# Weight splits and weight sums of a hybrid decoder layer, put in program order on their engines

## The chip, the cores and the metric

The kernel runs on one core of a Trainium2 chip. The metric is the device time of one execution in microseconds (us). Of several executions the median is given.

## The reference

One layer of a hybrid decoder, sequence 256, width D = 2048, FFN width 5632, all in float32. The change bears on the two SwiGLU FFNs; between them stands the mixer (differential attention beside a Mamba-2 scan).

```python
def swiglu(x, w_gate, w_up, w_down):
    return (jax.nn.silu(x @ w_gate) * (x @ w_up)) @ w_down
...
        f = swiglu(rms_norm(h, ffn1_pre_g[i]), ffn1_w_gate[i], ffn1_w_up[i], ffn1_w_down[i])
        h = h + 0.5 * rms_norm(f, ffn1_post_g[i])
        u = rms_norm(h, mix_pre_g[i])
...
        h = h + rms_norm(merged @ w_out[i], mix_post_g[i])
        f = swiglu(rms_norm(h, ffn2_pre_g[i]), ffn2_w_gate[i], ffn2_w_up[i], ffn2_w_down[i])
        h = h + 0.5 * rms_norm(f, ffn2_post_g[i])
```

## The kernel before, in words

**Products.** Every float32 weight block is loaded from HBM and split into two parts: hi, its value rounded to the multiply's input type (`split`, L130, an activation on ACT), and lo, the rest (L131, a subtraction on DVE that reads the block and hi). The activations are split likewise. A product is then three matmuls (hi by hi, hi by lo, lo by hi), in `gate_up` the lines L384, L385 and L386. L385 is the only one that reads a weight's lo. PE runs its instructions in the order in which they stand.

**FFN.** `gate_up` makes one block j of 256 columns of gate and up, j = 0 to 10 (NFF = 11). The blocks stand in groups (0 to 2, 3 to 5, 6 to 8, 9 and 10), and after each group a `project` multiplies by the down weights. For one j, eight pairs p of row blocks are gone through in an order: `ORDER_D` for the first j of a group, `ORDER` for the seven others (1, 2, 4, 5, 7, 8, 10).

```python
ORDER = (2, 0, 4, 1, 6, 3, 5, 7)
ORDER_D = (0, 2, 1, 4, 3, 6, 5, 7)
```

The pairs 2, 4 and 6 (SP) are *summed units*, S here, from j = 1 on: their 2x2 block product is made from seven products in place of eight, with sums of the weights and of the activations. The pairs 0, 1, 3, 5 and 7 are plain, N here. So a j with ORDER runs S N S N S N N N. An N unit has two weight splits of 128x1024, a and b, and 24 matmuls. An S unit has 21 matmuls and four splits: a (of raw columns 0 and 1), b (of the sums e0 and e1), d (of the sum e2, 128x512) and c (of raw columns 2 and 3, the last already replaced by a sum). Its products come in the order a, a, b, b, d, c, c; in the first S unit of a j the second product of a (`u0`) comes after d.

**Sums.** The class `Ahead` loads the raw block of an S unit into one of two buffers (`raw7`, L362) and has POOL make the sums with four adds of 128x512 (L366): e0 = raw0 + raw3, e1 = e0 + raw1, e2 = raw1 + raw3, raw3 = e1 + raw2. The e's lie in `wsum`, one of two buffers with the tags xc0 and xc1. `make` for the S unit after next is called where c of the present one has been split, which frees its raw buffer.

**Order.** A scheduler sets each engine's order from priorities: splits and sums stand under `high_priority(offset=AHEAD)` (AHEAD = 300), which lets them move forward; data dependencies and buffers hold. `issue_after(i)` adds an order edge: what is inside comes after i. The split results lie in a ring of four buffers for 128x1024 (tags w) and of two for 128x512 (tags one).

**Start.** While j = 0 runs, which has no S units, the squares of x are summed in `square1` (L520 to L525): four tiles, added on DVE into the first, which lies in xc0, and halved there twice. `scale1` then has PE sum it over the partitions (`ss`, L530, in PSUM), DVE scales (L110), POOL takes the power -1/2 (L111), and the result `pre_rstd` scales gate and up in L441 (ACT, silu) and L442 (DVE), which read the PSUM banks of a finished j.

Of the kernel before, what the change touches and what calls it, by code (L numbers as in the profile page):

```python
# [22 lines left out]
F32 = mybir.dt.float32  # L23
F32R = mybir.dt.float32r
AF = mybir.ActivationFunctionType
ALU = mybir.AluOpType
AX = mybir.AxisListType

P = 128
# [16 lines left out]
TT = NT * P  # L46
# [6 lines left out]
def decoder_layer(ctx: ExitStack, tc: tile.TileContext, x, x_t, cols, rows, post_g, wgu1, wd1, w_in,  # L53
                  w_in_t, w_dt, w_att, w_ssm, w_out, wgu2, wd2, out):
    nc = tc.nc
# [7 lines left out]
    tmp = E(name="tmp", bufs=12)  # L63
# [6 lines left out]
    def turn(tag, n):  # L70

        turns[tag] = (turns.get(tag, -1) + 1) % n
        return f"{tag}{turns[tag]}"
# [12 lines left out]
    ones = const.tile([P, P], F32, name="ones")  # L86
# [26 lines left out]
    loaded = [None]  # L113
    ahead = [AHEAD]
    queue = []

    def split(raw, shape, parts=1, before=None):
        tag = turn("one", 2) if shape[1:] == [S] else turn("w", 4)
        hi, lo = (wsplit.tile(shape, F32R, name=f"w_{p}", tag=f"{p}_{tag}") for p in ("hi", "lo"))
        k = shape[1] // parts  # L120
        with ExitStack() as st:
            if ahead[0] and not queue:
                st.enter_context(tc.high_priority(offset=ahead[0]))
            for i in queue.pop(0) if queue else ():
                st.enter_context(tc.issue_after(i.ins))
            for a in range(0, shape[1], k):
                js = slice(a, a + k)
                if before:
                    before(js)
                nc.scalar.activation(hi[:, js], raw[:, js], AF.Copy)  # L130
                nc.vector.tensor_tensor(out=lo[:, js], in0=raw[:, js], in1=hi[:, js].bitcast(F32), op=ALU.subtract)  # L131
        return hi, lo

    def matmul3(ps, sl, j, t, wh, wl, first, last):
# [5 lines left out]
    def project(xs, w, n, by_token=0):  # L140

        ps = [psm.tile([P, S], F32, name="acc", tag="m") for _ in range(NT)]
        tail = []
        for c in range(len(xs)):
            raw = raws.tile([P, 4, S], F32, name="raw", tag=turn("raw", 3))
            loaded[0] = nc.sync.dma_start(raw, w(n, c))
            sl = xs[c] = xs[c]() if callable(xs[c]) else xs[c]
            for b in range(2):  # L150
                hi, lo = split(raw[:, 2 * b:2 * b + 2], [P, 2, S])
                for jj in range(2):
                    j = 2 * b + jj
                    tail.append((sl, j, hi[:, jj], lo[:, jj], c + j == 0, c == len(xs) - 1 and j == 3))
            if c < len(xs) - by_token:
                for sl_, j, wh, wl, first, last in tail:
                    for t in range(NT):
                        matmul3(ps[t], sl_, j, t, wh, wl, first, last)
                tail = []
        for t in range(NT):  # L160
            for sl_, j, wh, wl, first, last in tail:
                matmul3(ps[t], sl_, j, t, wh, wl, first, last)
        return ps

    def project_t(xs, w, n):

        ps = [psm.tile([P, 2 * TT], F32, name="acc", tag="m") for _ in range(2)]
        for b in range(len(xs)):
            if b % 2 == 0:
                raw = raws.tile([P, 8, 256], F32, name="raw", tag=turn("raw", 3))  # L170
                nc.sync.dma_start(raw, w(n, b // 2))
            hi, lo = split(raw[:, 4 * (b % 2):4 * (b % 2) + 4], [P, 4, 256])
            sl = xs[b].rearrange("p j i t -> p j (i t)")
            for j in range(4):
                wf = [slice(f * P, (f + 1) * P) for f in range(2)]
                for f in range(2):
                    nc.tensor.matmul(ps[f], hi[:, j, wf[f]], sl[:, j], start=b + j == 0, stop=False)  # L177
                for f in range(2):
                    nc.tensor.matmul(ps[f][:, TT:], lo[:, j, wf[f]], sl[:, j, :TT], start=False,  # L179
                                     stop=b == len(xs) - 1 and j == 3)  # L180
        out = tmp.tile([P, 2, TT], F32, name="pt", tag="t2")
        for f in range(2):
            nc.scalar.activation(out[:, f], ps[f][:, TT:], AF.Copy)
            nc.vector.tensor_tensor(out=out[:, f], in0=ps[f][:, :TT], in1=out[:, f], op=ALU.add)
        return out
# [55 lines left out]
    def inv_rms(s1):  # L241

        rstd = const.tile([P, NT], F32, name="pre_rstd", tag="rstd")
        rsqrt(rstd, s1, D)
        return rstd
# [54 lines left out]
    class pair_slots:  # L300
# [8 lines left out]
        def make(self, p, src, gain):  # L309

            g = col[:, gain + 2 * p:gain + 2 * p + 2]
            kind = p in SP[:-1]
            if kind not in self.free:
                self.free[kind] = new_slot()
                sl, k = self.free[kind], 0
            else:
                sl, k = self.free.pop(kind), 2
            self.at0[p] = sl, k
            if p in SP:
                xg = self.xg[p] = tmp.tile([P, 2, TT], F32, name="xg", tag="t2")  # L320
                for i in range(2):
                    nc.scalar.activation(xg[:, i], src[:, i], AF.Copy, scale=g[:, i:i + 1])
                fill(sl, k, xg)
            else:
                self.at[p] = sl, k
                for i in range(2):
                    nc.scalar.activation(sl[:, k + i, 0], src[:, i], AF.Copy, scale=g[:, i:i + 1])
                    nc.vector.scalar_tensor_tensor(
                        out=sl[:, k + i, 1], in0=src[:, i], scalar=g[:, i:i + 1],
                        in1=sl[:, k + i, 0].bitcast(F32), op0=ALU.mult, op1=ALU.subtract)  # L330
# [15 lines left out]
    class Ahead:  # L346
# [6 lines left out]
        def make(self):  # L353
            if len(self.made) == 2 or not self.units:
                return
            j, p = self.units.pop(0)


            raw = hpool.tile([P, 4, S], F32, name="raw7", tag=turn("h", 2))
            e = tmp.tile([P, 3, S], F32, name="wsum", tag=turn("xc", 2), bufs=1)  # L360
            with tc.high_priority(offset=AHEAD), tc.issue_after(self.behind.ins) if self.behind else nullcontext():
                nc.sync.dma_start(raw, self.w[j, p])  # L362
            with tc.high_priority(offset=AHEAD):
                for o, a, b in ((e[:, 0], raw[:, 0], raw[:, 3]), (e[:, 1], e[:, 0], raw[:, 1]),
                                (e[:, 2], raw[:, 1], raw[:, 3]), (raw[:, 3], e[:, 1], raw[:, 2])):
                    nc.gpsimd.tensor_tensor(out=o, in0=a, in1=b, op=ALU.add)  # L366
            self.made.append((raw, e))

        def take(self):
# [145 lines left out]
    sq = []  # L515

    def square1(c):

        sq.append(tmp.tile([P, 4, TT], F32, name="sq", tag=f"xc{min(c, 1)}", bufs=1))
        nc.scalar.activation(sq[c], xT[:, 2 * c:2 * c + 2], AF.Square)  # L520
        if c:
            nc.vector.tensor_tensor(out=sq[0], in0=sq[0], in1=sq[c], op=ALU.add)
        if c == 3:
            for k in (2, 1):
                nc.vector.tensor_tensor(out=sq[0][:, :k], in0=sq[0][:, :k], in1=sq[0][:, k:2 * k], op=ALU.add)  # L525

    def scale1():
        s1 = psm.tile([P, NT], F32, name="ss", tag="m")
        for t in range(NT):
            nc.tensor.matmul(s1[:, t:t + 1], sq[0][:, 0, t * P:(t + 1) * P], ones[:, 0:1], start=True, stop=True)  # L530
        return inv_rms(s1)

    def fetch1(p):
# [5 lines left out]
        return None if p else raw0  # L539

    steps1 = {i: lambda c=c: square1(c) for c, i in enumerate((1, 2, 4, 5))}
    update = ffn(x1, {**steps1, 7: scale1}, wgu1, wd1, 0, lambda t: x[t * P:(t + 1) * P], fetch1)

# [38 lines left out]
    raw = raws.tile([P, 16, P], F32, name="raw", tag=turn("raw", 3))  # L582
# [301 lines left out]
    for n in range(4):  # L884
        sg = gate(W_GS + n)
        ps = proj(done[6:8], lambda n, c: w_ssm[n, 6 + c], n)
        for t in range(NT):
            a = part[:, t, n * S:(n + 1) * S]
# [6 lines left out]
    for n in range(4):  # L895
# [3 lines left out]
        for t in range(NT):  # L899
            a = part[:, t, n * S:(n + 1) * S]  # L900
# [89 lines left out]
```

## Time and profile before

| | us |
|---|---|
| median of 3 runs (2847.24 to 2847.94) | 2847.88 |
| the profiled execution | 2847.33 |
| its span, first to last instruction | 2845.6 |
| TensorE (PE) busy | 2782.3 |
| VectorE (DVE) busy | 1971.5 |
| ScalarE (ACT) busy | 1435.5 |
| GpSimd (POOL) busy | 538.5 |

In the profile PE is TensorE's matmuls, PEld its weight loads, SP the engine whose queue issues most loads. A row of a timeline is an instruction or a few alike in succession; its duration is given before the engine's name, and in square brackets stands how long the engine was idle before it and what ended that. A matmul's end is modelled, so that rows of PE overlap; what counts is from start to start. "L131" is line 131 of the kernel before; in the changed kernel the same line is L135, and L130, L366, L441 and L442 are L134, L372, L447 and L448.

### The profile page before, as it was taken

Reading aid. Unit: us, or ns where it says so; the run is one execution under the profiler, and the core shown is the slowest. Engines: PE = TensorE matmul, PEld = TensorE weight load, DVE = VectorE, ACT = ScalarE, POOL = GpSimd, SP = SyncE. Lnnn points to the kernel's source line nnn. Section 1 sums busy time; section 2 is a strip of 40 time slices with the busy share of each in tenths; the row PEclk is TensorE's granted clock in tenths of the full one; section 3 lists DMA queues with packets and bytes.
Section 4 is the critical chain, followed back from the end, with each engine's and each line's share of the span. In section 5 each row is a group of like instructions: output and inputs, shape, how many; then the busy total and the mean of one; then the engine's idle time right before and its main releaser. Section 6 shows DMA issues by size and latency. Waiting matters only on the chain. (4 is left out here: it accounts for less than half of the span.)

```text
span 2845.6 us, 33737 instructions
## 1 busy us (share of the span) xinstructions
PE 2782.3 (98%) x13120; PEld 2307.5 (81%) x13120; DVE 1971.5 (69%) x2311; ACT 1435.5 (50%) x1822; POOL 538.5 (19%) x377
## 2 busy tenths in 40 slices
PE   8999999999999999999999999999999999999998
PEld 6787787887788888888888888888878887877877
DVE  7857857867778776777765555545578658678576
ACT  6544544545565555545444444444465445445454
POOL 2504305213012110111100000000024124034030
PEclk9999999999999999999999999999999999999999
DMA  6554555555555555555554445555565554545554
GB/s 243 204 193 177 199 186 192 192 180 211 186 195 181 188 185 187 190 181 189 195 186 168 177 171 185 197 195 192 185 227 187 196 189 178 207 177 193 195 187 165
DMA packets 77984, 541.49 MB, mean 190 GB/s; under 512 B 8768, under 2 KB 8912, under 8 KB 14080
## 3 DMA queue, kind: packets, MB, share of 16 engines
q1 hardware_dynamic: 73152, 519.08, 50.8%
q0 software_dynamic: 4528, 20.09, 2.0%
q8 instruction: 103, 1.69, 0.2%
q14 instruction: 57, 0.47, 0.0%
q10 hardware_dynamic: 144, 0.17, 0.0%
HBM read 532.94 MB, written 6.36 MB: 190 GB/s over the span
## 5 line engine op out<-in xcount | busy, mean ns | idle before, releaser
L131 DVE TENSOR_TENSOR w_lo<-raw,w_hi 128x1024 fp32r<-128x1024 f32 x978 | 1267.5, 1307 | 660.8 <-ACT w_hi L130 653.0
L130 ACT ACTIVATE w_hi<-raw 128x1024 fp32r<-128x1024 f32 x978 | 1023.9, 1057 | 918.0 <-PE acc L138 577.7
L136 PE MATMUL acc<-w_hi,slot 128*128 128x512 f32 x1856 | 729.1, 393 | 0.8 <-DVE slot L201 0.2
L137 PE MATMUL acc<-w_lo,slot 128*128 128x512 f32 x1856 | 722.9, 389 | 0.9 <-DVE w_lo L131 0.9
L138 PE MATMUL acc<-w_hi,slot 128*128 128x512 f32 x1856 | 719.8, 389 | 0.0
L136 PEld LDWEIGHTS acc<-w_hi,slot 128*128 128x128 f32 x1856 | 348.5, 188 | 78.3 <-ACT slot L193 4.6
L137 PEld LDWEIGHTS acc<-w_lo,slot 128*128 128x128 f32 x1856 | 348.7, 188 | 74.2 <-DVE w_lo L131 1.7
L177 PE MATMUL acc<-slot,w_hi 128*128 128x512 f32 x1280 | 407.8, 399 | 0.2 <-ACT zs L770 0.2
L138 PEld LDWEIGHTS acc<-w_hi,slot 128*128 128x128 f32 x1856 | 348.5, 188 | 73.0
L366 POOL TENSOR_TENSOR wsum<-raw 128x512 f32<-128x512 f32 x120 | 197.1, 1663 | 918.8 <-DMA raw<-in_wgu 775.5
L384 PE MATMUL gu<-w_hi,slot 128*128 128x512 f32 x928 | 363.0, 392 | 7.5 <-ACT w_hi L130 7.5
L385 PE MATMUL gu<-w_lo,slot 128*128 128x512 f32 x928 | 363.4, 392 | 3.5 <-DVE w_lo L131 3.5
L386 PE MATMUL gu<-w_hi,slot 128*128 128x512 f32 x928 | 362.3, 390 | 0.0
L179 PEld LDWEIGHTS acc<-slot,w_lo 128*128 128x128 f32 x1280 | 240.5, 188 | 56.1
L130 ACT ACTIVATE w_hi<-wsum 128x512 fp32r<-128x512 f32 (+1 forms) x120 | 101.5, 846 | 305.8 <-POOL wsum L366 259.1
L179 PE MATMUL acc<-slot,w_lo 128*128 128x256 f32 x1280 | 252.9, 278 | 0.0
L131 DVE TENSOR_TENSOR w_lo<-wsum,w_hi 128x512 fp32r<-128x512 f32 (+1 forms) x120 | 169.3, 1420 | 119.2 <-ACT w_hi L130 119.1
L385 PEld LDWEIGHTS gu<-w_lo,slot 128*128 128x128 f32 x928 | 174.9, 188 | 43.8 <-DVE w_lo L131 7.6
L384 PEld LDWEIGHTS gu<-w_hi,slot 128*128 128x128 f32 x928 | 174.7, 188 | 44.0 <-ACT w_hi L130 7.7
L386 PEld LDWEIGHTS gu<-w_hi,slot 128*128 128x128 f32 x928 | 174.8, 188 | 36.1
L177 PEld LDWEIGHTS acc<-slot,w_hi 128*128 128x128 f32 x1280 | 196.6, 189 | 4.3 <-issue 2.4
L385 PE MATMUL gu<-w_lo,sums 128*128 128x512 f32 x420 | 168.1, 401 | 26.0 <-DVE w_lo L131 25.6
(227 smaller groups left out, 2168.8 us busy)
## 6 DMA issues: line engine op xcount, KB each, us to landing
raw<-in_wgu SPq DMA_DIRECT2D x175, 1024.0 KB, 4.8
raw<-in_wd SPq DMA_DIRECT2D x88, 1024.0 KB, 4.8
raw<-in_w_in SPq DMA_DIRECT2D x80, 1024.0 KB, 4.8
raw<-in_w_in_t SPq DMA_DIRECT2D x80, 1024.0 KB, 4.8
raw<-in_w_ssm SPq DMA_DIRECT2D x32, 1024.0 KB, 4.7
raw<-in_w_att SPq DMA_DIRECT2D x16, 1024.0 KB, 4.8
raw<-in_w_out SPq DMA_DIRECT2D x16, 1024.0 KB, 4.7
dec<-acsD POOLq DMA_DIRECT2D x16, 512.0 KB, 5.1
```

The costliest lines, as they stand in the source:

```text
L130: nc.scalar.activation(hi[:, js], raw[:, js], AF.Copy)
L131: nc.vector.tensor_tensor(out=lo[:, js], in0=raw[:, js], in1=hi[:, js].bitcast(F32), op=ALU.subtract)
L136: nc.tensor.matmul(ps, xh, wh, start=first, stop=False)
L137: nc.tensor.matmul(ps, xh, wl, start=False, stop=False)
L138: nc.tensor.matmul(ps, xl, wh, start=False, stop=last)
L177: nc.tensor.matmul(ps[f], hi[:, j, wf[f]], sl[:, j], start=b + j == 0, stop=False)
L179: nc.tensor.matmul(ps[f][:, TT:], lo[:, j, wf[f]], sl[:, j, :TT], start=False, stop=b == len(xs) - 1 and j == 3)
L366: nc.gpsimd.tensor_tensor(out=o, in0=a, in1=b, op=ALU.add)
L384: nc.tensor.matmul(bank[k], xh, wh, start=done[k] == 1, stop=False)
L385: nc.tensor.matmul(bank[k], xh, wl, start=False, stop=False)
L386: nc.tensor.matmul(bank[k], xl, wh, start=False, stop=done[k] == count[k])
```

## The change

It does three things. In `split`, each hi split is issued after the last hi split, and each lo split after the last lo split, in the order in which the program calls `split`, which is the order of the products. In `Ahead.make`, each of POOL's adds is issued after the last one. In `square1`, the last halving add writes to a new tile `sqs`, of another tag (t2), and `scale1` reads that in place of xc0.

```diff
--- before.py
+++ after.py
@@ -113,6 +113,8 @@
     loaded = [None]
     ahead = [AHEAD]
     queue = []
+    split_last = {}
+    sum_last = [None]
 
     def split(raw, shape, parts=1, before=None):
         tag = turn("one", 2) if shape[1:] == [S] else turn("w", 4)
@@ -123,12 +125,15 @@
                 st.enter_context(tc.high_priority(offset=ahead[0]))
             for i in queue.pop(0) if queue else ():
                 st.enter_context(tc.issue_after(i.ins))
+            for i in split_last.values():
+                st.enter_context(tc.issue_after(i.ins))
             for a in range(0, shape[1], k):
                 js = slice(a, a + k)
                 if before:
                     before(js)
-                nc.scalar.activation(hi[:, js], raw[:, js], AF.Copy)
-                nc.vector.tensor_tensor(out=lo[:, js], in0=raw[:, js], in1=hi[:, js].bitcast(F32), op=ALU.subtract)
+                split_last["hi"] = nc.scalar.activation(hi[:, js], raw[:, js], AF.Copy)
+                split_last["lo"] = nc.vector.tensor_tensor(out=lo[:, js], in0=raw[:, js],
+                                                           in1=hi[:, js].bitcast(F32), op=ALU.subtract)
         return hi, lo
 
     def matmul3(ps, sl, j, t, wh, wl, first, last):
@@ -363,7 +368,8 @@
             with tc.high_priority(offset=AHEAD):
                 for o, a, b in ((e[:, 0], raw[:, 0], raw[:, 3]), (e[:, 1], e[:, 0], raw[:, 1]),
                                 (e[:, 2], raw[:, 1], raw[:, 3]), (raw[:, 3], e[:, 1], raw[:, 2])):
-                    nc.gpsimd.tensor_tensor(out=o, in0=a, in1=b, op=ALU.add)
+                    with tc.issue_after(sum_last[0].ins) if sum_last[0] else nullcontext():
+                        sum_last[0] = nc.gpsimd.tensor_tensor(out=o, in0=a, in1=b, op=ALU.add)
             self.made.append((raw, e))
 
         def take(self):
@@ -521,13 +527,14 @@
         if c:
             nc.vector.tensor_tensor(out=sq[0], in0=sq[0], in1=sq[c], op=ALU.add)
         if c == 3:
-            for k in (2, 1):
-                nc.vector.tensor_tensor(out=sq[0][:, :k], in0=sq[0][:, :k], in1=sq[0][:, k:2 * k], op=ALU.add)
+            sq.append(tmp.tile([P, TT], F32, name="sqs", tag="t2"))
+            nc.vector.tensor_tensor(out=sq[0][:, :2], in0=sq[0][:, :2], in1=sq[0][:, 2:], op=ALU.add)
+            nc.vector.tensor_tensor(out=sq[4], in0=sq[0][:, 0], in1=sq[0][:, 1], op=ALU.add)
 
     def scale1():
         s1 = psm.tile([P, NT], F32, name="ss", tag="m")
         for t in range(NT):
-            nc.tensor.matmul(s1[:, t:t + 1], sq[0][:, 0, t * P:(t + 1) * P], ones[:, 0:1], start=True, stop=True)
+            nc.tensor.matmul(s1[:, t:t + 1], sq[4][:, t * P:(t + 1) * P], ones[:, 0:1], start=True, stop=True)
         return inv_rms(s1)
 
     def fetch1(p):
```

ACT, from N1's b split (`raw_2355`) before the second S unit of j = 4 in FFN 1. S2 is `raw7_2141` with the sums `wsum_2142`, S3 is `raw7_2320` with `wsum_2321`, and `raw_2434` is the N unit between them. Before:

```order
L130 ACTIVATE w_hi_2390<-raw7_2141 128x1024
L130 ACTIVATE w_hi_2361<-raw_2355 128x1024
L130 ACTIVATE w_hi_2394<-wsum_2142 128x1024
L130 ACTIVATE w_hi_2476<-wsum_2321 128x512
L130 ACTIVATE w_hi_2402<-raw7_2141 128x1024
L130 ACTIVATE w_hi_2436<-raw_2434 128x1024
L130 ACTIVATE w_hi_2440<-raw_2434 128x1024
L130 ACTIVATE w_hi_2468<-raw7_2320 128x1024
L130 ACTIVATE w_hi_2472<-wsum_2321 128x1024
```

After, where the number of a tile is one higher:

```order
L134 ACTIVATE w_hi_2362<-raw_2356 128x1024
L134 ACTIVATE w_hi_2391<-raw7_2142 128x1024
L134 ACTIVATE w_hi_2395<-wsum_2143 128x1024
L134 ACTIVATE w_hi_2399<-wsum_2143 128x512
L134 ACTIVATE w_hi_2403<-raw7_2142 128x1024
L134 ACTIVATE w_hi_2437<-raw_2435 128x1024
L134 ACTIVATE w_hi_2441<-raw_2435 128x1024
L134 ACTIVATE w_hi_2469<-raw7_2321 128x1024
L134 ACTIVATE w_hi_2473<-wsum_2322 128x1024
L134 ACTIVATE w_hi_2477<-wsum_2322 128x512
```

S2's a stood ahead of N1's b, and S3's d (`w_hi_2476`) ahead of S2's c (`w_hi_2402`), while S2's own d stood further ahead, out of this piece. Now a, b, d, c of S2, the N unit, and then a, b, d of S3 follow one another.

DVE at the same place, before:

```order
L131 TENSOR_TENSOR w_lo_2391<-raw7_2141,w_hi_2390 128x1024
L131 TENSOR_TENSOR w_lo_2362<-raw_2355,w_hi_2361 128x1024
L442 SCALAR_TENSOR_TENSOR c_g1_2170<-c_u1_2172,pre_rstd_477,c_g1_2170 128x512
L131 TENSOR_TENSOR w_lo_2395<-wsum_2142,w_hi_2394 128x1024
L131 TENSOR_TENSOR w_lo_2477<-wsum_2321,w_hi_2476 128x512
L131 TENSOR_TENSOR w_lo_2403<-raw7_2141,w_hi_2402 128x1024
L131 TENSOR_TENSOR w_lo_2437<-raw_2434,w_hi_2436 128x1024
L131 TENSOR_TENSOR w_lo_2441<-raw_2434,w_hi_2440 128x1024
L131 TENSOR_TENSOR w_lo_2469<-raw7_2320,w_hi_2468 128x1024
```

After:

```order
L135 TENSOR_TENSOR w_lo_2363<-raw_2356,w_hi_2362 128x1024
L135 TENSOR_TENSOR w_lo_2392<-raw7_2142,w_hi_2391 128x1024
L135 TENSOR_TENSOR w_lo_2396<-wsum_2143,w_hi_2395 128x1024
L135 TENSOR_TENSOR w_lo_2400<-wsum_2143,w_hi_2399 128x512
L135 TENSOR_TENSOR w_lo_2404<-raw7_2142,w_hi_2403 128x1024
L135 TENSOR_TENSOR w_lo_2438<-raw_2435,w_hi_2437 128x1024
L135 TENSOR_TENSOR w_lo_2442<-raw_2435,w_hi_2441 128x1024
L135 TENSOR_TENSOR w_lo_2470<-raw7_2321,w_hi_2469 128x1024
L135 TENSOR_TENSOR w_lo_2474<-wsum_2322,w_hi_2473 128x1024
L135 TENSOR_TENSOR w_lo_2478<-wsum_2322,w_hi_2477 128x512
```

DVE's lo splits follow the same order as ACT's hi splits. Counted over the whole program, 237 lo splits stood out of their order before, and 27 do after.

POOL at the start of its sums: `raw7_429` is the first S unit of j = 1 (pair 2), `raw7_493` the second. Before:

```order
L366 TENSOR_TENSOR wsum_494<-raw7_493 128x512 x2
L366 TENSOR_TENSOR wsum_494<-wsum_494,raw7_493 128x512
L366 TENSOR_TENSOR raw7_493<-wsum_494,raw7_493 128x512
L366 TENSOR_TENSOR wsum_430<-raw7_429 128x512 x2
L366 TENSOR_TENSOR wsum_430<-wsum_430,raw7_429 128x512
L111 TENSOR_TENSOR pre_rstd_477<-rs_v_478,mhalf_99 128x2
L366 TENSOR_TENSOR raw7_429<-wsum_430,raw7_429 128x512
```

After (tiles one higher):

```order
L372 TENSOR_TENSOR wsum_431<-raw7_430 128x512
L372 TENSOR_TENSOR wsum_431<-wsum_431,raw7_430 128x512
L372 TENSOR_TENSOR wsum_431<-raw7_430 128x512
L372 TENSOR_TENSOR raw7_430<-wsum_431,raw7_430 128x512
L372 TENSOR_TENSOR wsum_495<-raw7_494 128x512
L372 TENSOR_TENSOR wsum_495<-wsum_495,raw7_494 128x512
L372 TENSOR_TENSOR wsum_495<-raw7_494 128x512
L372 TENSOR_TENSOR raw7_494<-wsum_495,raw7_494 128x512
L111 TENSOR_TENSOR pre_rstd_478<-rs_v_479,mhalf_99 128x2
```

The first unit's sums now come ahead of the second's, and within each unit e1 ahead of e2; the power of L111 comes after both. In all 60 units e1 and e2 have changed places. On PE, the products of the first S unit of j = 1 in FFN 1 were mixed with those of the unit behind it and now stand straight; elsewhere its order is the same but for three places of a few rows. The mixer's instructions do not move.

## Rows read from the trace of the kernel before

**Rows 1.** The page, part 1: busy time, share of the span, instructions.
```profile
PE 2782.3 (98%) x13120; PEld 2307.5 (81%) x13120; DVE 1971.5 (69%) x2311; ACT 1435.5 (50%) x1822; POOL 538.5 (19%) x377
```

**Rows 2.** Waits of PE: line, line waited for: us in total, times, longest.
```profile
PE gu L385 <- DVE w_lo L131: 29.0, 36, 1.5
PE gu L384 <- ACT w_hi L130: 12.6, 2, 7.5
```

**Rows 3.** Waits of all engines, the row for ACT and POOL's sums.
```profile
ACT w_hi L130 <- POOL wsum L366: 259.1, 61, 5.7
```

**Rows 4.** Timeline of ACT in j=4: start, us, instruction, [idle before <-releaser].
```profile
266.29 1.04 ACT L130 ACTIVATE w_hi<-wsum 128x1024 fp32r<-128x1024 f32 x1
271.27 0.63 ACT L130 ACTIVATE w_hi<-wsum 128x512 fp32r<-128x512 f32 x1 [3.94 <-POOL wsum L366]
```

**Rows 5.** Timeline of DVE in j=4, x2: two instructions in one row.
```profile
270.01 4.02 DVE L131 TENSOR_TENSOR w_lo<-wsum,w_hi 128x1024 fp32r<-128x1024 f32 x2
273.95 5.72 DVE L131 TENSOR_TENSOR w_lo<-raw,w_hi 128x1024 fp32r<-128x1024 f32 x4
...
298.82 2.34 DVE L131 TENSOR_TENSOR w_lo<-raw,w_hi 128x1024 fp32r<-128x1024 f32 x2
301.09 1.27 DVE L194 TENSOR_TENSOR slot<-tp,slot 128x512 fp32r<-128x512 f32 x2
302.29 1.21 DVE L131 TENSOR_TENSOR w_lo<-raw,w_hi 128x1024 fp32r<-128x1024 f32 x1
```

**Rows 6.** Timeline of PE in j=4.
```profile
274.25 0.39 PE L386 MATMUL gu<-w_hi,sums 128*128 128x512 f32 x1
274.47 0.39 PE L384 MATMUL gu<-w_hi,sums 128*128 128x512 f32 x1
276.31 0.50 PE L385 MATMUL gu<-w_lo,sums 128*128 128x512 f32 x1 [1.45 <-DVE w_lo L131]
276.65 0.40 PE L386 MATMUL gu<-w_hi,sums 128*128 128x512 f32 x1
```

**Rows 7.** Timeline of POOL in j=4; source line L366: ns min/median/max.
```profile
267.45 3.79 POOL L366 TENSOR_TENSOR wsum<-raw 128x512 f32<-128x512 f32 x2 [8.96 <-DMA raw<-in_wgu]
...
273.55 1.62 POOL L366 TENSOR_TENSOR raw<-wsum,raw 128x512 f32<-128x512 f32 x1
...
L366 POOL TENSOR_TENSOR wsum<-raw x120: 1267/1642/2340, 42.1 to 2756.6; 128x512 f32<-128x512 f32 x120
```

**Rows 8.** Timelines at j=1: POOL, then DVE, then ACT.
```profile
42.13 3.52 POOL L366 TENSOR_TENSOR wsum<-raw 128x512 f32<-128x512 f32 x2 [39.19 <-DMA raw<-in_wgu]
...
55.31 3.48 POOL L366 TENSOR_TENSOR wsum<-raw 128x512 f32<-128x512 f32 x2 [5.72 <-PE ss L530]
...
59.98 1.17 POOL L111 TENSOR_TENSOR pre_rstd<-rs_v,mhalf 128x2 f32<-128x2 f32 x1
...
31.00 0.41 DVE L525 TENSOR_TENSOR sq<-sq 128x256 f32<-128x256 f32 x1
...
55.27 0.16 DVE L110 TENSOR_SCALAR rs_v<-ss 128x2 f32<-128x2 f32 x1 [4.60 <-PE ss L530]
...
63.51 1.28 ACT L441 ACT_TABLE_LOAD   x1
64.80 0.69 ACT L441 ACTIVATE sg<-gu,pre_rstd 128x512 f32<-128x512 f32 x1
```

**Rows 9.** Windows at j=1: length, busy (instructions) PE PEld DVE ACT POOL, PEclk, DMA.
```profile
55.88:61.16 5.28, 0.17 (x2) 0.00 (x1) 2.75 (x3) 1.79 (x3) 5.28 (x5) 0.69 0.00 0
61.16:64.71 3.55, 3.55 (x8) 2.80 (x9) 3.51 (x2) 2.26 (x2) 1.24 (x1) 0.51 0.00 0
```

**Rows 10.** The page, part 6: issues, KB each, us to landing.
```profile
raw<-in_wgu SPq DMA_DIRECT2D x175, 1024.0 KB, 4.8
```

**Rows 11.** Windows of j=4 and j=5, columns as in rows 9.
```profile
259.60:306.31 46.71, 43.63 (x193) 34.77 (x191) 39.99 (x39) 24.00 (x28) 19.20 (x12) 1.00 0.49 180
306.31:350.40 44.09, 42.95 (x192) 35.01 (x191) 37.43 (x35) 23.95 (x27) 18.71 (x12) 1.00 0.54 194
```

## The prediction

> **What bounds the kernel now.** I read the page's first part, then TensorE's waits, then the two stretches where it waits. PE is busy for 98% of the span [rows 1], so nothing that only shortens DVE, ACT or POOL can pay except by ending a PE wait. The waits by line [rows 2] leave little to look for: 29.0 us in 36 waits of L385 for a lo split, and 12.6 us in 2 waits of L384 for a hi split, the longer (7.5) at the kernel's start, before any weight is there. The other is at 56 us. Both are in the FFNs' `gate_up`. The list for ACT names what lies behind them: 61 times, 259.1 us in all, a hi split waits for POOL's weight sums [rows 3]. There are 60 summed units, so that is about once for each.
>
> **Where one such wait comes from** (second summed unit of j=4, S2; its first matmul is 15 x 0.227 ahead of 274.47, at 271.07). ACT splits S2's b at 266.29 and then stands 3.94 us until 271.27 for a 128x512 sum [rows 4]. The order of ACT in the section on the change says whose: the d of S3, the next summed unit, which PE needs some 12 us later. S2's own c, ready since its load, is queued behind it, and its lo split on DVE starts at 273.95 [rows 5]. PE multiplies by c's hi at 274.47 and gets c's lo at 276.31, with 1.45 us counted as idle [rows 6]. The matmul after it comes 0.34 us later where 0.22 to 0.23 is usual, and 274.47 to 276.65 is 2.18 us for what takes 0.45: 1.73 lost for 1.45 counted, so each wait costs 0.28 us more than the list says. All 36 together: 29.0 + 36 x 0.28 = 39.1 us. That POOL is late for d is no fault of POOL's speed: it starts S3's sums at 267.45 and ends them at 275.17 [rows 7], 6 us before S3's start at 281.3 (10.2 us after S2's, by 21 and 24 matmuls at 0.227, without what that stretch loses).
>
> **The change, step by step.** No instruction is added but one DVE add in another shape; everything is order.
>
> *Start.* In before, POOL does the second unit's sums (42.13) ahead of the first's, which wait until 55.31 for the `ss` matmul that reads the squares in the same buffer [rows 8]. PE stands through 55.88:61.16 (5.28 us, two matmuls' ends of busy time in it), and in 61.16:64.71 its granted clock is 0.51, the lower of its two levels (1.2 GHz), so that eight matmuls take 3.55 us where 8 x 0.227 = 1.82 is usual [rows 9]. Lost: 5.28 + 1.73 = 7.0. After, the sums' buffer is free when DVE's last add has read it, where before it ended at 31.41, and POOL does the first unit first: both units' sums take eight adds, 10 us at 1.27 each and 14 at the 3.52 for two that the row at 42.13 shows, so from 42 they are done by 52 to 56, and the first by 49, ahead of 55.09. What is late next is a PSUM bank. The first unit's fifth product, `u0`, is due 12 matmuls after 55.09, at 57.8, and needs the bank that L441 reads first. That chain is L110 at 55.27 with 0.16, the power on POOL 1.17, L441 0.69 (and a table load of 1.28 that can run beside the power) [rows 8]: 57.5 to 58.6. I take 0.5 for it, between nothing and 0.8. Gain 6.5.
>
> *Order of splits.* Each of the 36 waits is of the kind above, or of the a split ahead of the other unit's b. In the new order c is split in its turn, so the gain is bounded by 39.1 above, and below by what the same two engines can deliver. That is the disputed term, since the wait for POOL stays and only moves: S's b now heads both queues, with d, c and the next units' splits behind it, and all of PE behind those. Three rows price it. Alone, two lo splits of 128x1024 take 2.27 us from start to next start, so 1.13 each, and a small DVE operation 0.60 [rows 5]. Alone, a POOL add takes 1.27 [rows 7]. Beside each other, DVE takes 3.94 us for a large and a small split (1.73 alone), and POOL 6.0 us from 267.45 for three adds (3.8 alone): about twice as long each. A run of the new order by hand, T being S1's first matmul: S1's c is split by T-0.2 and frees the buffer, the raw weights land 4.8 us later [rows 10], POOL works from T+4.7 to T+13.2 (four adds at 2.1), and DVE meanwhile does N's b (2.25), S2's a and b (2.25 each) and d (1.7), from T+4.4 to T+12.9, and c alone from there to T+14.3. PE wants c's lo at T+10.2 and 16 matmuls, T+13.8. Late by 0.5; b, d and all the others are in time, as their sums were made for them a unit earlier. A j with ORDER holds 19 large and 3 small lo splits and 13 small operations on DVE (35 in the window of j=5), 21.5+1.8+7.8 = 31.1 us alone, and 12 adds, 15.2 alone: 46.3 of work for a PE period of 3x4.76 + 5x5.44 + 0.8 = 42.3. They must overlap. By the window of j=5 (DVE 37.43 and POOL 18.71 busy in 44.09 [rows 11], so at least 12.05 together) 46.3 of work in 44.09 means at least 1.18 us of work in an overlapped us; by the rows at 270 it is 0.44 + 0.63 = 1.07. With POOL overlapped for the 25 us that twelve contended adds take, a j needs 46.3 - 0.18x25 = 41.8 or 46.3 - 0.07x25 = 44.5. So the rest that stays per j lies between 0 and 2.2; I take 0.8, above the 0.5 of the hand run and near the lower price, because the hand run has no idle and j=5 is a measurement of a whole period. There are 14 such j (seven in each FFN; the first j of a group has its splits made during the projection before): 11.2 stays, with ends at 0 and 31.
>
> *Order of sums.* The adds of a unit become e0, e1, e2, raw3. The second sum e1 no longer waits for e2, so b is ready one add earlier and d one later; both are made several us ahead. Nothing.
>
> *Last add into its own buffer.* One DVE add of 128x256 as before. Nothing but the start above.
>
> **The sum.** 2847.3 (the profiled execution) - 6.5 - 39.1 + 11.2 = 2812.9. The median of the runs stands 0.55 above that execution, so 2813.
>
> **Rivals.** *A: DVE and POOL are the bound.* Each j keeps j=5's 44.09. 1.8 x 14 = 25 stays: 2847.9 - 45.6 + 25 = 2827. For it: DVE's splits at double length wherever POOL works. Against: in j=5 DVE also stood idle for 6.7 us, which the new order takes away.
>
> *B: the waits come back elsewhere, or the order matters less than it looks.* Only the start pays, 2841, or not even that, 2848. Against: S2's c is ready and short, and only its place in the queue holds it.
>
> *C: slower, by the head of the queue.* If POOL's e1 comes later than b's turn, ACT holds all later splits, loads' buffers come free later, and POOL starts later still. It decides when a unit's sums end some 6 us later than now (275.17 for S3, against b's first matmul at 281.3 + 6 x 0.227 = 282.7, less a hi split of 1.06). If each of 60 units is late by 0.9 us, that is 54: 2847.9 - 45.6 + 54 = 2856. Against: the order by hand makes POOL earlier, not later, as c's splits free the raw buffer sooner.
>
> *D: DVE and POOL exclude each other wholly.* Then a j takes 46.3, and 4.0 x 14 = 56 stays: 2858. The Trainium skill, "SBUF — State Buffer", section "Who interferes with whom", says that GpSimd reads through the port pair that DVE's second input uses, and that the pair is an exclusive lock. By that rule alone D would be the forecast. The window of j=5 disagrees in size: 46.3 of work ran in 44.09, with 6.7 of DVE's time idle.
>
> **How the numbers follow.** Forecast 0.62, A 0.22, B 0.06, C 0.05, D 0.05. The forecast's own range is 2799 (all of both terms) to 2820. With A it is 2799 to 2834, which leaves out B, C, D and the far end of A. A measurement of this kernel tells about 0.2% (5.7 us) from no change. Faster: forecast, A and a third of B, 0.86; same: the rest of B and the near parts of C and D, 0.07; slower: 0.07.
>
> **What the profile after would show.** Right: POOL's first unit before 51 us, no wait of PE near 56, and its granted clock high there; ACT's waits for POOL far below 259.1; L385's waits for lo splits down from 29.0 to some 5 to 8, on products of c. A: the same, with those waits at 15 to 25 and DVE hardly idle in a j. B: as many waits, on b or on N's. C or D: L384 waiting for b's hi with a sum as its releaser, or j's of 46 us and more. I would be wrong mostly by the rest per j: DVE has next to no idle time left to absorb an error in the price of its contended split.

## The result, and the profile after

The changed kernel takes 2821.9 us (2820.9 to 2822.9, 4 runs) against 2847.9: a ratio of 0.9908, 95% interval 0.9891 to 0.9926. It is faster by 26 us where 35 was forecast. The profiled execution took 2822.5, its span is 2820.8.

The page's first part and the waits of PE, as [rows 1, 2] show them for before:

```profile
PE 2776.0 (98%) x13120; PEld 2307.2 (82%) x13120; DVE 2034.9 (72%) x2311; ACT 1443.4 (51%) x1822; POOL 648.5 (23%) x377
...
PE gu L391 <- DVE w_lo L135: 15.9, 21, 2.5
PE gu L390 <- ACT w_hi L134: 7.4, 1, 7.4
```

L391 and L390 are the L385 and L384 of before. The waits for lo splits fell from 29.0 us in 36 to 15.9 in 21, and the wait of 5.1 us for a hi split at 56 us is gone. POOL has the same 377 instructions and is busy for 648.5 us where it was 538.5, and DVE for 63 us more. Next come the row of ACT's waits for sums, against the 259.1 us of [rows 3], and the adds by source line (shortest, median and longest in ns), against a median of 1642 for the first form in [rows 7]:

```profile
ACT w_hi L134 <- POOL wsum L372: 14.9, 19, 1.1
...
L372 POOL TENSOR_TENSOR wsum<-raw x120: 1281/2277/2381, 35.6 to 2733.5; 128x512 f32<-128x512 f32 x120
L372 POOL TENSOR_TENSOR wsum<-wsum,raw x60: 1353/2159/2340, 36.9 to 2731.4; 128x512 f32<-128x512 f32 x60
L372 POOL TENSOR_TENSOR raw<-wsum,raw x60: 1300/2157/2177, 40.6 to 2735.9; 128x512 f32<-128x512 f32 x60
```

ACT hardly stands any more for a sum that is not due. While it stood in before, DVE soon had nothing to split either, and many of POOL's adds ran undisturbed. Now DVE is at work whenever POOL adds, and the median add of the first form takes 2.28 us.

**The summed unit of [rows 4 to 7] again.** S2 of j = 4 starts at 263.58 here. The timelines of POOL, DVE and PE around it:

```profile
260.22 1.82 POOL L372 TENSOR_TENSOR wsum<-raw 128x512 f32<-128x512 f32 x1 [7.20 <-DMA raw<-in_wgu]
262.12 2.16 POOL L372 TENSOR_TENSOR wsum<-wsum,raw 128x512 f32<-128x512 f32 x1
264.24 2.28 POOL L372 TENSOR_TENSOR wsum<-raw 128x512 f32<-128x512 f32 x1
266.59 1.61 POOL L372 TENSOR_TENSOR raw<-wsum,raw 128x512 f32<-128x512 f32 x1
...
259.67 3.46 DVE L135 TENSOR_TENSOR w_lo<-raw,w_hi 128x1024 fp32r<-128x1024 f32 x2
263.05 4.02 DVE L135 TENSOR_TENSOR w_lo<-wsum,w_hi 128x1024 fp32r<-128x1024 f32 x2
266.99 5.71 DVE L135 TENSOR_TENSOR w_lo<-raw,w_hi 128x1024 fp32r<-128x1024 f32 x4
...
264.94 0.39 PE L390 MATMUL gu<-w_hi,sums 128*128 128x512 f32 x1
265.42 0.50 PE L391 MATMUL gu<-w_lo,sums 128*128 128x512 f32 x1
...
266.68 0.39 PE L390 MATMUL gu<-w_hi,sums 128*128 128x512 f32 x1
267.12 0.50 PE L391 MATMUL gu<-w_lo,sums 128*128 128x512 f32 x1
...
267.70 0.40 PE L390 MATMUL gu<-w_hi,sums 128*128 128x512 f32 x1
269.35 0.50 PE L391 MATMUL gu<-w_lo,sums 128*128 128x512 f32 x1 [1.25 <-DVE w_lo L135]
```

DVE now has no pause at all: N's b and S2's a, then S2's b and d, then c. But until POOL ends at 268.20 a large split takes about double, and PE starts on the lo parts of b (265.42), d (267.12) and c (269.35) late. None of these splits waits for a sum. The row at 263.05 holds two splits, b and d, which a narrower window shows one by one:

```profile
263.05 2.31 DVE L135 TENSOR_TENSOR w_lo<-wsum,w_hi 128x1024 fp32r<-128x1024 f32 x1
265.29 1.78 DVE L135 TENSOR_TENSOR w_lo<-wsum,w_hi 128x512 fp32r<-128x512 f32 x1
```

POOL's add of 264.24 ends at 266.52, 1.16 us behind the end of b. Then d ends at 267.07, 0.55 behind that add, and POOL's last add at 268.20, 1.13 behind d. So the two engines take turns, one whole operation at a time: each ends about its own length after the other's end. A split of 1.13 us and an add of 1.27, each by itself, take 2.24 in turn, from 263.05 to 265.29.

Not every DVE operation takes part. At 324.23 one that reads one of its two inputs from PSUM (`gu`) runs within an add of POOL and takes its usual 0.68; the twenty of that line take 0.676 to 0.683 us.

```profile
323.31 2.16 POOL L372 TENSOR_TENSOR raw<-wsum,raw 128x512 f32<-128x512 f32 x1
324.23 0.68 DVE L432 TENSOR_TENSOR u<-gu,c_g 128x512 f32<-128x512 f32 x1
```

The windows of j = 4 and j = 5, with the columns of [rows 9], against 46.71 and 44.09 in [rows 11]:

```profile
253.35:298.05 44.70, 43.31 (x193) 34.88 (x191) 41.84 (x38) 24.82 (x28) 24.65 (x12) 1.00 0.53 188
298.05:341.18 43.13, 42.67 (x193) 35.10 (x192) 39.46 (x34) 23.70 (x26) 25.10 (x12) 1.00 0.59 209
```

DVE is busy for 41.84 of 44.70 and 39.46 of 43.13, and POOL for 25 us in each.

**The start.** POOL's first unit is done at 42.0, its second at 47.5, and the first summed unit runs without a pause from 58.65. But PE met a new wait before it, in the last pair of j = 0. Timelines of DVE, POOL and PE, and the window behind the wait:

```profile
39.31 1.58 DVE L344 TENSOR_TENSOR xf<-xg 128x128 f32<-128x128 f32 x2
40.81 1.38 DVE L344 TENSOR_TENSOR xf<-xf,xg 128x128 f32<-128x128 f32 x1
42.12 1.51 DVE L348 TENSOR_TENSOR sums<-xg,sums 128x256 fp32r<-128x256 f32 x1
43.55 1.37 DVE L344 TENSOR_TENSOR xf<-xg,xf 128x128 f32<-128x128 f32 x1
...
40.62 1.42 POOL L372 TENSOR_TENSOR raw<-wsum,raw 128x512 f32<-128x512 f32 x1
42.01 1.34 POOL L372 TENSOR_TENSOR wsum<-raw 128x512 f32<-128x512 f32 x1
43.42 1.35 POOL L372 TENSOR_TENSOR wsum<-wsum,raw 128x512 f32<-128x512 f32 x1
...
48.60 0.65 PE L391 MATMUL gu<-w_lo,slot 128*128 128x512 f32 x1 [2.54 <-DVE w_lo L135]
...
48.60:52.04 3.44, 3.44 (x9) 2.69 (x9) 3.44 (x4) 0.00 (x0) 0.00 (x0) 0.53 0.71 229
```

DVE's small sums of the activations, 0.28 us for a 128x128 one in before, take 1.37 beside POOL's adds: each of the last three rows starts just behind the start of an add and ends 0.15 to 0.28 us behind its end. They stand ahead of a lo split, and PE waits 2.54 us for that. Its granted clock behind the wait is 0.53, the lower of its two levels, until 52.04: eight matmuls take 3.44 us there, where 8 x 0.227 = 1.82 is usual. In all, the 35 matmuls behind the one at 45.68 take 12.4 us in place of 7.9, so the new wait costs 4.4. The transposes late in j = 1, here and then in before:

```profile
89.66 1.04 PE L218 MATMUL tp<-ident,sg 128*128 128x128 f32 x8
...
94.57 1.03 PE L213 MATMUL tp<-ident,sg 128*128 128x128 f32 x8
```

Up to there 4.9 us are gained, 0.9 of them already in the first 24 us, where the loads of x are issued a little earlier. That the change does this is not shown: the kernel without POOL's sums, further below, keeps the other edits and starts the same matmuls 0.7 us later than the changed kernel.

### The profile page after: what moved, and what is told of

It is laid out like the page before. It is cut to its first block, busy times and chain, and to the rows that moved or that the text cites. A ratio compares the mean times of both kernels' runs of the same rounds, so it can differ in the third digit from the quotient of the medians.

```text
span 2820.8 us, 33781 instructions
## 1 busy us (share of the span) xinstructions
PE 2776.0 (98%) x13120; PEld 2307.2 (82%) x13120; DVE 2034.9 (72%) x2311; ACT 1443.4 (51%) x1822; POOL 648.5 (23%) x377
## 5 line engine op out<-in xcount | busy, mean ns | idle before, releaser
L135 DVE TENSOR_TENSOR w_lo<-raw,w_hi 128x1024 fp32r<-128x1024 f32 x978 | 1335.0, 1376 | 672.5 <-ACT w_hi L134 666.3
L372 POOL TENSOR_TENSOR wsum<-raw 128x512 f32<-128x512 f32 x120 | 248.2, 2068 | 769.6 <-DMA raw<-in_wgu 734.1
L390 PE MATMUL gu<-w_hi,slot 128*128 128x512 f32 x928 | 363.4, 392 | 7.4 <-ACT w_hi L134 7.4
L391 PE MATMUL gu<-w_lo,slot 128*128 128x512 f32 x928 | 362.9, 391 | 2.7 <-DVE w_lo L135 2.7
L390 PEld LDWEIGHTS gu<-w_hi,slot 128*128 128x128 f32 x928 | 174.9, 189 | 43.9 <-ACT w_hi L134 7.8
L391 PEld LDWEIGHTS gu<-w_lo,slot 128*128 128x128 f32 x928 | 175.0, 189 | 40.8 <-DVE w_lo L135 4.5
L391 PE MATMUL gu<-w_lo,sums 128*128 128x512 f32 x420 | 167.0, 398 | 13.9 <-DVE w_lo L135 13.2
L135 DVE TENSOR_TENSOR w_lo<-wsum,w_hi 128x1024 fp32r<-128x1024 f32 x120 | 166.5, 1427 | 13.0 <-ACT w_hi L134 13.0
L390 PE MATMUL gu<-w_hi,sums 128*128 128x512 f32 x420 | 163.7, 390 | 0.0
```

The costliest lines, as they stand in the source:

```text
L135: split_last["lo"] = nc.vector.tensor_tensor(out=lo[:, js], in0=raw[:, js], in1=hi[:, js].bitcast(F32), op=ALU.subtract)
L372: sum_last[0] = nc.gpsimd.tensor_tensor(out=o, in0=a, in1=b, op=ALU.add)
L390: nc.tensor.matmul(bank[k], xh, wh, start=done[k] == 1, stop=False)
L391: nc.tensor.matmul(bank[k], xh, wl, start=False, stop=False)
```

## The experiments

All were timed beside runs of the kernel before on the same chip (medians of 2847.2 to 2848.5 us), and each ratio is to those.

**The chain of the splits alone** (label `e1_splits_alone`): POOL's adds without a chain, squares in xc0.

```diff
-                    with tc.issue_after(sum_last[0].ins) if sum_last[0] else nullcontext():
+                    with nullcontext():
...
-            sq.append(tmp.tile([P, TT], F32, name="sqs", tag="t2"))
+            sq.append(sq[0][:, 0])
```

> The chain of the splits alone: the adds on POOL keep the order of the kernel before, and the squares end in xc0. Theory (the gain after the start comes from the order of the splits): only the start is lost again, 2822 + 5 = 2827, and PE's waits for lo splits stay near 21. Rival (the order of the sums frees the queue, the splits' order alone does half): 2834 or more, with some 30 waits.

Measured: 2827.8, ratio 0.9928 (0.9911 to 0.9944), and 21 waits of L391, 13.6 us. The chain of the splits is worth 20 of the 26 us by itself.

**The other two parts without it** (`e2_sums_squares`).

```diff
-            for i in split_last.values():
-                st.enter_context(tc.issue_after(i.ins))
```

> The other half: sums chained and squares in their own buffer, splits in the scheduler's own order. Theory: the start gains its 5 us and nothing else does, 2843, with PE's 36 waits for lo splits and ACT's 61 waits for sums as before. Rival: with the sums in order the splits come right by themselves, 2835 or less.

Measured: 2871.2, ratio 1.0082 (1.0067 to 1.0097): slower by 23.5 us, which neither theory had. Waits of PE, and of ACT for sums:

```profile
PE gu L389 <- DVE w_lo L133: 43.8, 58, 1.5
PE gu L388 <- ACT w_hi L132: 13.2, 19, 7.6
...
ACT w_hi L132 <- POOL wsum L370: 351.9, 60, 6.7
```

ACT waits 5.9 us a unit in place of 4.2. So the old queue, with the next unit's d at its head, pays for the one thing that the chain of sums does in every unit: d's sum becomes the third add. The next run asks that.

**d's sum second again** (`e10_sums_d_first`), otherwise as the run before.

```diff
-                for o, a, b in ((e[:, 0], raw[:, 0], raw[:, 3]), (e[:, 1], e[:, 0], raw[:, 1]),
-                                (e[:, 2], raw[:, 1], raw[:, 3]), (raw[:, 3], e[:, 1], raw[:, 2])):
+                for o, a, b in ((e[:, 0], raw[:, 0], raw[:, 3]), (e[:, 2], raw[:, 1], raw[:, 3]),
+                                (e[:, 1], e[:, 0], raw[:, 1]), (raw[:, 3], e[:, 1], raw[:, 2])):
```

> As the run of sums and squares alone (2871), but with the adds chained as e0, e2, e1, raw3, so that d's sum is the second add again. Theory (without the chain of the splits the next unit's d stands ahead of c, so an add more ahead of d's sum holds c longer): 2848 less the 5 us of the start, 2843, with ACT's waits for sums back near 259 us. Rival (chaining the sums as such, or doing the first unit first, costs the time): 2865 to 2872.

Measured: 2843.2, ratio 0.9983 (0.9973 to 0.9993), with the waits at the old size:

```profile
PE gu L389 <- DVE w_lo L133: 30.0, 34, 1.8
...
ACT w_hi L132 <- POOL wsum L370: 260.9, 59, 5.6
```

One add's place in the order is worth 28 us under the old queue. In both runs every wait of ACT for a sum stands before a split of 128x512, a d. This bears out what held c: the sum of the next unit's d.

**No chain of sums** (`e3_no_sum_chain`), the first edit of the first run alone.

> The changed kernel without the chain of the sums: on POOL only e1 and e2 of all 60 units change places back, nothing moves elsewhere. Theory: POOL is several us early, so 2822 within 1. Rival (b's sum is on the path and comes one contended add of 2.2 us later): up to 19 waits longer by 1 us, 2830 to 2840.

Measured: 2822.2, ratio 0.9910 (0.9895 to 0.9925), 20 waits of L391. With the splits in order the place of d's sum costs nothing.

**Squares in xc0** (`e4_no_squares`), the second edit of the first run alone.

> The changed kernel with the squares ending in xc0 again, so that POOL's first sums wait for the ss matmul near 55 us. Theory: the stall of the start is back, 2822 + 5 = 2827, and no new 2.5 us wait in the last pair of j = 0, as POOL no longer runs beside DVE there. Rival (what the free buffer gains, the new wait at 46 us takes back): 2822 to 2823.

Measured: 2828.7, ratio 0.9935 (0.9920 to 0.9949). The longest wait of L391 is 1.3, so the 2.54 at 46 us is not there, and L390 waits twice for a hi split (10.9 us in all, 12.6 in before) and once, for 1.6 us, for L448, which reads a finished bank. The free buffer is worth 6 to 7 us against the two kernels that lack it; by the transposes of j = 1, which start at 95.33 here, 5.7 of them fall in the start, though 0.75 of these stand in the first 24 us, ahead of the edited add.

**What remains: POOL's sums left out** (`e6_no_adds`). The four adds and their tile go, and the splits read the raw block:

```diff
...
-                bh, bl = split(e[:, 0:2], [P, 2, S])
-                dh, dl = split(e[:, 2], [P, S])
+                bh, bl = split(raw[:, 0:2], [P, 2, S])
+                dh, dl = split(raw[:, 2], [P, S])
```

> The changed kernel without POOL's sums: b, d and c are split from the raw block, so the summed units multiply other numbers. It is the floor for everything that POOL does to the splits, by waits or by slowing DVE. Remaining excess of the summed units is 23 us and the start holds about 4.5: 2822 - 27 = 2795 by both theories; 2815 or more would say that the rest is neither.

**All adds run, their results unused** (`e9_adds_unused`): the same two lines, and the last add writes to e[:, 0].

> The changed kernel with all four adds run, but b, d and c split from the raw block, so no split waits for a sum (the result is another; the last add writes into wsum). Contention theory: DVE is slowed as before, 2822 within 3, with L391 waits near 20. Queue theory (later splits stand behind b's wait for POOL): all of it is gone, 2795 to 2800.

**Two adds of four** (`e7_two_adds`): d from raw as above, and the last two adds left out.

> The changed kernel with two of four adds per unit (e0 and e1; d and c are split from the raw block, so the result is another). Contention theory (DVE loses about half of the time in which POOL adds): half of POOL's time, and as the lateness has a threshold less than half of the rest, 2798 to 2805. Queue theory (b waits for POOL's e1 at the head of the queue): e1 is as late as before, 2815 to 2822.

Measured: 2796.7 without the adds (ratio 0.9823, 0.9808 to 0.9838), 2823.2 with all four run for nothing (0.9914, 0.9898 to 0.9931), 2797.1 with two (0.9823, 0.9808 to 0.9837). In all three the products are of other numbers. In the second no split waits for a sum, and PE waits just as in the changed kernel; in the first and third the list has no wait of PE for a lo split of a weight at all. The rows of the second:

```profile
PE gu L391 <- DVE w_lo L135: 16.3, 21, 2.6
PE gu L390 <- ACT w_hi L134: 7.6, 1, 7.6
```

So the queue theory falls: the rest is DVE slowed by POOL's adds, and half of the adds cost PE nothing, so that it is not in proportion to them. The windows of j = 4 and j = 5 without the adds give DVE's own work:

```profile
248.01:290.38 42.37, 42.37 (x192) 35.17 (x191) 32.05 (x35) 24.20 (x27) 0.00 (x0) 1.00 0.56 199
290.38:332.66 42.28, 42.28 (x192) 35.10 (x191) 31.34 (x33) 23.68 (x26) 0.00 (x0) 1.00 0.60 211
```

The periods are PE's own, 42.3 to 42.4. DVE is busy for 32.05 and 31.34, against 41.84 and 39.46 with POOL adding: twelve adds on POOL cost DVE 9.8 and 8.1 us, 0.68 to 0.82 each. The windows do not hold quite the same operations (38 and 34 on DVE against 35 and 33); over the whole kernel DVE is busy for 2034.9 us against 1861.5, which is 0.72 for each of the 240 adds.

**The adds on DVE** (`e8_sums_on_dve`): emitted in `Ahead.make` for the unit loaded one call earlier, so behind the next unit's c.

```diff
...
+                with tc.issue_after(split_last["lo"].ins):
+                    split_last["lo"] = nc.vector.tensor_tensor(out=o, in0=a, in1=b, op=ALU.add)
```

> The four adds of a unit moved from POOL to DVE, behind the c split of the unit before it, in the chain of the lo splits. Contention theory: twelve adds of 0.6 us on 31 us of DVE work make 38 for a period of 42.3, DVE runs at its own pace and the rest goes: 2796 to 2803, faster than both kernels. Rival (DVE becomes full, or stands at an add whose load has not landed): 2822 to 2835.

Measured: 2805.5, ratio 0.9855 (0.9840 to 0.9870), faster than both kernels and slower than expected. The list has no wait of PE for a lo split, but its weight loads, which run ahead of the products, have 26 (first row, waits of PEld). Below it the timelines of DVE and PE behind a summed unit:

```profile
PEld gu L400 <- DVE w_lo L135: 13.8, 26, 0.8
...
260.18 1.22 DVE L135 TENSOR_TENSOR w_lo<-raw,w_hi 128x1024 fp32r<-128x1024 f32 x1
261.31 0.68 DVE L379 TENSOR_TENSOR wsum<-raw 128x512 f32<-128x512 f32 x1
...
263.36 0.69 DVE L379 TENSOR_TENSOR raw<-wsum,raw 128x512 f32<-128x512 f32 x1
263.97 3.49 DVE L135 TENSOR_TENSOR w_lo<-raw,w_hi 128x1024 fp32r<-128x1024 f32 x3
...
263.90 1.07 PE L399 MATMUL gu<-w_hi,slot 128*128 128x512 f32 x4
264.81 0.39 PE L399 MATMUL gu<-w_hi,sums 128*128 128x512 f32 x1
265.25 0.50 PE L400 MATMUL gu<-w_lo,slot 128*128 128x512 f32 x1
```

Four adds, 2.66 us from 261.31 to 263.97, stand ahead of the plain unit's a lo split, which begins at 263.97. PE's own order runs four products with a's hi first (263.90), and the first with a's lo still comes 0.44 us behind the matmul ahead of it, where 0.23 is usual. That is an order again, which the next run changes.

**The adds on DVE, one split later** (`e12_dve_adds_later`).

```diff
...
                 ah, al = split(raw[:, 0:2], [P, 2, S])
+                if coming and j:
+                    coming.sum()
                 bh, bl = split(raw[:, 2:4], [P, 2, S])
```

> All four adds on DVE again, one split later: behind the a split of the plain unit that follows, no longer ahead of it. Theory (the 9 us that the adds on DVE lost to the floor are the plain unit's a lo split, held behind 2.7 us of adds): 2796 to 2800. Rival (DVE is too full with 38 us of work a period, wherever the adds stand): 2803 to 2808.

**Two adds on each engine** (`e11_two_and_two`): e0 and e1 on POOL, e2 and raw3 on DVE, at the place that `e8_sums_on_dve` has for its adds.

> The changed kernel with e0 and e1 on POOL, early, and e2 and raw3 on DVE behind the c split of the unit before, so that each engine adds half. Contention theory: POOL's two adds were free (2797 with the other two left out), and DVE has room for 6 x 0.6 = 3.6 us in a period of 42.3: 2796 to 2802. Rival (any work more on DVE is paid on PE, as with all four adds on DVE, 2805 against 2797): 2801 to 2806.

Measured: 2796.0 for the adds placed later (ratio 0.9819, 0.9803 to 0.9835), 2798.7 for two and two (0.9827, 0.9812 to 0.9841). Both are about as fast as the kernel without any adds, and 23 to 26 us faster than the changed kernel. DVE's windows with all twelve adds on it:

```profile
247.99:290.39 42.40, 42.40 (x192) 35.18 (x191) 38.55 (x47) 24.21 (x27) 0.00 (x0) 1.00 0.54 199
290.39:332.67 42.28, 42.28 (x192) 35.11 (x191) 37.85 (x46) 23.68 (x26) 0.00 (x0) 1.00 0.59 211
```

DVE is busy for 38.55 and 37.85: 6.5 us more than without the adds, 0.54 each, less than the 0.68 to 0.82 that it loses to the same add on POOL (over the whole kernel 0.55 against 0.72).

## Why the prediction was right, and where its sizes were off

**The mechanism held.** The next unit's d ahead of c cost the time (the run with d's sum second shows it from the other side), and with the splits in order the waits for sums all but vanish. The rival that nothing changes and the one of a blocked head of the queue are out: 14.9 us of ACT's waits for sums are left, and no L390 waits for a sum. The time that rival D gave is out too, as j = 4 and j = 5 take 44.7 and 43.1 us and not 46.3; its rule is another matter, see below.

**The sizes were less good.** The 2821.9 lie 2 us above the forecast's own range of 2799 to 2820, and inside 2799 to 2834 only because that takes in rival A. (With the ends of the rest per j, 0 and 31 us, the terms make some 2802 to 2833, so the narrower range does not follow from them.) L391's waits of 15.9 us fall where A put them, at 15 to 25, and not at the forecast's 5 to 8. By the starts of the same matmuls in the two profiled executions, which are 24.8 us apart, 4.9 were gained up to late in j = 1, 8.8 in the rest of FFN 1, 2.1 in the mixer and 9.0 in FFN 2. Beyond j = 1 the order of the splits paid 17.8 us in the FFNs, where 39.1 - 11.2 = 27.9 stood.

**The start gained 4.9 us up to late in j = 1, where 6.5 was put for the start alone.** The chain of the PSUM bank was rightly small; PE has no wait there. What the step missed stands earlier: POOL's adds, taken to start at 42 us, run from 35.6 and slow DVE's small sums to five times their length ahead of a lo split that PE needs. That took back 4.4 us. The step asked what is late next on POOL, ACT and PSUM, and not what DVE does while POOL runs.

**The rest per j was the term that was mis-sized.** It was put at 0.8 us in 14 periods, 11.2, between ends of 0 and 2.2. The runs give 44.70 - 42.37 = 2.3 for j = 4 and 43.13 - 42.28 = 0.85 for j = 5. Of the 21 waits, one is the start's 2.54 and one of 0.15 stands in the load-bound first pairs; of the 19 others six are like that of j = 4 (1.25 to 1.27 us counted, in j = 4, 7 and 10 of both FFNs) and 13 are of 0.40 to 0.47, as in j = 5. If each costs as in j = 4 or j = 5, that makes 6 x 2.3 + 13 x 0.8 = 24 us where 11.2 stood. The hand run had named place and size for j = 5 (c's lo, late by 0.5; 0.46 is counted). It was wrong to take one period for all 14, and to leave out the first j of a group: six of the 13 lie there. In the j after such a first one, two plain units and not three separate its first summed unit from the last one, and POOL adds without a pause from 235.83 to 253.02. That this is why j = 4 is worse was argued from the rows and not tried.

**The rival of DVE and POOL as the bound** was right that DVE beside POOL is the cause of what remains, and too dear: 2827 by j = 5 of before, whose 44.09 still held the wrong order. The measured time lies between it and the forecast.

**Rival D was dismissed for a wrong reason.** The Trainium skill, "SBUF — State Buffer", section "Who interferes with whom", names the port pair that DVE's second input and GpSimd share and calls it an exclusive lock. The rows agree, operation by operation: beside an add of POOL a DVE operation whose inputs both lie in SBUF (the on-chip memory that holds the weights) takes some 1.1 us longer whatever its size, from 0.28 to 1.38, from 0.68 to 1.78 and from 1.21 to 2.31. The prediction's 46.3 us per j counted all 13 small DVE operations as excluded. By the kernel's text eleven of these read an input from PSUM (`gu` or `tp`), and such operations keep their 0.68 us beside POOL. Without 11 x 0.60 = 6.6 us the work that must take turns is 39.7 us in a period of 42.3: it fits, and what costs PE time is splits that have to let adds pass shortly before they are due. So the 46.3 in 44.09 is no evidence against the lock. Of the prediction's two rates, 1.07 us of work in an overlapped us is what taking turns gives (1.13 + 1.27 in 2.24), and 1.18 holds operations that do not take turns as well.

**The mixer** was counted at nothing and gave some 2 us: 1347.7 us from the first wait behind FFN 1 to that ahead of FFN 2 in before, 1345.7 after. Two waits of its first projections for lo splits, at 767.89 and 771.30 in before (0.52 and 0.36 us counted), are gone.

## What to carry to other kernels

When several engines each serve a queue in order, a result that is not due soon must not stand ahead of one that is due now: look in the list of waits for an engine that waits often for an input, and ask what ready work is queued behind it. Before an elementwise operation is put on GpSimd to relieve VectorE, measure what VectorE loses while both run; here doing it on VectorE itself cost less, once it stood behind the split that was due first. When two engines take turns, count only the operations that take part, and look at the short ones: they lose as many us as the long ones. An order edge is worth as much as the queue around it: the place of one sum in its chain cost 28 us with the splits out of order and nothing with them in order.

## What the runs showed of the hardware

A 128x512 float32 add took 0.68 us on DVE. On POOL it took 1.27 us alone, 1.34 to 1.42 beside DVE operations of 128x128 and 128x256, 1.61 beside a split of 128x512 and 2.2 to 2.3 beside splits of 128x1024. In these rows POOL and a DVE operation with both inputs in SBUF take turns, one whole operation at a time, so that a DVE operation takes some 1.1 us longer at every size (128x128: 0.28 and 1.38 us; 128x1024: 1.21 and 2.31). DVE operations that read one input from PSUM took 0.68 us beside POOL and alone. Over the whole kernel DVE's busy time grew by 0.72 us for each such add on POOL and by 0.55 for each on DVE itself.
